# Dilated attention's logits from rounded parts stacked over 128 rows, and a new order of the branches in the mix stage of a two-block model

## The chip, the cores and the metric

One core of a Trainium2 chip runs the whole program as one launch. The metric is device time in microseconds of an execution; lower is better. The kernel before took 2573.86 us (median of 3 runs, 2573.66 to 2575.83).

Engines are named as in the profile: PE (TensorE, matrix products), ACT (ScalarE), DVE (VectorE), POOL (GpSimd), SP (SyncE, which here only issues DMAs). Each engine takes its instructions in a fixed order and waits at the first that isn't ready. ACTq, SPq and POOLq are the same engines issuing DMAs.

## The reference

A first block of two layers (three kinds of attention and memory each) is followed by a second block, on 512 tokens of width 1024 in float32. The change lies in the second block's mixing layer:

```python
def hybrid_layer_2(x, mem, ...):
    x = x + 0.5 * swiglu_ffn(rmsnorm(x, ffn1_norm), ffn1_w_in, ffn1_w_down)
    u = rmsnorm(x, mix_norm)
    u_ssm, q, k, v, xq, g_ssm, g_attn, g_mem = jnp.split(u @ w_in, cuts, axis=-1)
    y_ssm = jax.nn.gelu(s5_scan(u_ssm, ...))
    glu_a, glu_b = jnp.split(y_ssm @ ssm_w_glu, 2, axis=-1)
    br_ssm = glu_a * jax.nn.sigmoid(glu_b)
    br_attn = dilated_mixture_attention(q, k, v, rel_table) @ attn_w_up
    br_mem = memory_cross_attention(xq, rmsnorm(mem, mem_norm), xattn_w_kv) @ xattn_w_up
    merged = sigmoid(g_ssm) * br_ssm + sigmoid(g_attn) * br_attn + sigmoid(g_mem) * br_mem
    x = x + merged @ w_out
    return x + 0.5 * swiglu_ffn(rmsnorm(x, ffn2_norm), ffn2_w_in, ffn2_w_down)
```

The dilated attention has three patterns of four heads of width 64. Each query sees keys at distances 0, d, 2d, ... with d = 1, 4, 16; logits get a bias by distance. The three patterns' outputs of a head are weighted by their softmax denominators ("shares").

## The kernel before

Values are kept transposed (features on partitions, 512 tokens along the row). A large product is made of float32 operands split into a rounded high part and the rest (`hi`, `lo`, type fp32r), and of three products of 512 columns, hi x hi, hi x lo, lo x hi (`three`, lines 302 to 304). Weights come in pieces of 512 KB: SP issues the load into `raw` (line 265, two buffers), ACT rounds it (`whi`, line 270), DVE subtracts (`wlo`, line 271), three buffers each.

The mix stage runs three strands side by side, which `together` interleaves by cost: the main strand `mix_products` (projections, then gates and branch products, 256 of 1024 output features at a time), the state space (`side`, from `ssm`), and `attention` (memory's two halves, `cross`, and the dilated patterns, `dilated`, in turn). A gate is a projection and a tanh into an `fr` buffer (line 1152, four buffers). `gated` multiplies a gate with its branch and keeps the sum of branches in HBM (`mxd`, POOL's queue): place 0 writes it, place 1 reads, adds and writes it, and with `mh` the sum is rounded into the operand of the last product instead. Before, the order of branches is memory, dilated attention, and, after both side strands have ended, the state space.

`dilated` goes through 24 blocks of 128 queries and two heads (three patterns, two pairs `m`, four blocks). Per block: two logits products (one for each head, 64 rows of Q against 64 rows of K, plain fp32, line 1478), bias and minimum on DVE (line 1484), exponential on ACT (line 1486), transposes on PE (line 506), a copy on ACT (line 1492) and the value products (line 1497). An fp32 product shows as two instructions in the trace. Outputs go to HBM (`od`), maxima and sums too (`std`).

`shares` loads the statistics (`sh`), makes the weights `wt`, transposes them on PE, writes them to HBM (`wd`), loads them back over 64 partitions each (`row<-wd`, twelve DMAs on ACT's queue, four `row` buffers) and adds up the three outputs (`fr<-od`). `reload` brings a branch's input back from HBM, `fr<-yd` for memory and `fr<-sd` for the state space: a load into `fr`, an ACT cast (line 1286) and a DVE subtraction (line 1287) into `xk`.

The program's statements are scheduled ahead of time, by priority and buffers, into one fixed order for each engine.

Of the kernel before, what the change touches and what calls it, by code (L numbers as in the profile page):

```python
# [8 lines left out]
F32 = mybir.dt.float32  # L9
# [225 lines left out]
class Prog:  # L235
# [953 lines left out]
    def mix_products(self, W):  # L1189

        have = self.have
        for x in (self.cross_q(W, 0), self.dilated_qkv(W, 0), self.cross_q(W, 1), self.dilated_qkv(W, 1), self.dilated_qkv(W, 2)):
            yield from x
        x = None
        for c in range(4):
            th = self.gate(W[21 + c])
            yield 10.0
            if x is None:
                while "c1" not in have:
                    yield 0.0  # L1200
                x = self.reload(self.load_cross)
            br = self.featmajor(self.A["wxup"][c], x, nk=4)
            self.gated(c, th, br, 0)
            yield 5.0
        for c in range(4):
            th = self.gate(W[17 + c])
            yield 10.0
            while c == 0 and "oa" not in have:
                yield 0.0
            br = self.featmajor(self.A["wup"][c], self.oa, nk=2)  # L1210
            self.gated(c, th, br, 1)
            yield 3.0

    def together(self, main, streams):

        due = [0.0] * len(streams)
        for cost in main:
            for i, (gen, per) in enumerate(streams):
                due[i] += cost
                while due[i] >= per or cost == 0.0:  # L1220
                    if not next(gen, None):
                        due[i] = min(due[i], 10.0)
                        break
                    due[i] -= per
                    if cost == 0.0:
                        break
        for gen, _ in streams:
            for _ in gen:
                pass

    def mix(self):
# [4 lines left out]
        with tc.tile_pool(name="mix", bufs=1, reuse_waits="tile") as ap:  # L1236
            self.ap = ap
            with tc.tile_pool(name="ssm", bufs=1, reuse_waits="tile") as sp:
                side = self.ssm(W, sp)
                next(side)  # L1240
                z, self.hT = self.hT, self.h8(ap, "hn")
                for k in range(8):
                    q = self.row()
                    nc.vector.tensor_add(q, z[0][k].bitcast(F32), z[1][k].bitcast(F32))
                    nc.vector.tensor_mul(q, q, self.R)
                    self.split(self.hT[0][k], self.hT[1][k], q)
                self.have = set()
                self.cross_kv()
                self.together(self.mix_products(W), [(side, self.per), (self.attention(), self.aper)])
            with tc.tile_pool(name="fin", bufs=1, reuse_waits="tile") as fp:  # L1250
                mh = [[self.t(fp, [P, S], F32R, tag=f"mh{i}{d}") for d in range(8)] for i in range(2)]
                y = self.reload(self.load_ssm)
                for c in range(4):
                    pg = self.gate(W[13 + c])
                    br = []
                    for m in range(2):
                        a, b = self.featmajor(self.A["wglu"][2 * c + m], y, nk=4)
                        t = self.fr()
                        nc.scalar.activation(t, b, AF.Tanh)
                        nc.vector.scalar_tensor_tensor(t, t, 1.0, a, op0=ALU.add, op1=ALU.mult)  # L1260
                        br.append(t)
                    self.gated(c, pg, br, 2, mh)
# [35 lines left out]
    def xk(self, dt=F32R):  # L1298
        return self.t(self.ap, [P, 2, S], dt, tag="xk", bufs=6)
# [115 lines left out]
    def dilated_qkv(self, W, p):  # L1415
        nc, ap = self.nc, self.ap
        w, at, nb = self.BANDS[p]
        bias = self.m4(shape=(4, nb))
        for h in range(4):
            v = self.bd[4 * p + h][127:127 + P * (w - 1)].rearrange("(p w) -> p w", w=w - 1)  # L1420
            nc.sync.dma_start(bias[:, h, :], v[:, :nb])
        qk = []
        for x in range(2):
            ps = self.featmajor(W[2 + 3 * x + p], self.hT)
            X = self.m4()
            for m in range(2):
                src, dst = ps[m], X[:, m, :]
                if p:
                    src = src.rearrange("p (i r) -> p r i", r=4)
                    dst = dst.rearrange("p (r i) -> p r i", r=4)  # L1430
                nc.scalar.mul(dst, src, 0.125 if x == 0 else 1.0)
            qk.append(X)
            yield 10.0
# [30 lines left out]
    def dilated(self, p):  # L1464
# [6 lines left out]
        for m in range(2):  # L1471
            o = self.av()
            for b in range(NB):
                k0, n = (b * P, P) if p or b == 0 else ((b - 1) * P, 256)
                ps = [self.lt() for _ in range(2)]
                for e in range(2):
                    r = slice(64 * e, 64 * e + 64)
                    nc.tensor.matmul(ps[e][:, :n], Q[r, m, b * P:(b + 1) * P], K[r, m, k0:k0 + n], start=True, stop=True)  # L1478
                L = self.row()
                for e in range(2):  # L1480
# [3 lines left out]
                    nc.vector.tensor_tensor_reduce(Le, ps[e][:, :n], bias[:, h, nb - n:], op0=ALU.add, op1=ALU.min,  # L1484
# [21 lines left out]
    def shares(self):  # L1506
# [25 lines left out]
        acc = []  # L1532
        for p in range(3):
            for m in range(2):
                o, t = self.fr(), self.row()
# [4 lines left out]
                if p == 0:  # L1540
                    nc.vector.tensor_mul(o, o, t)
                    acc.append(o)
# [4 lines left out]
        oa = [self.xk() for _ in range(2)]  # L1547
# [212 lines left out]
    def ssm(self, W, sp):  # L1760
        nc, ap = self.nc, self.ap
        srow = lambda: self.t(sp, [P, S], tag="srow", bufs=6)
# [158 lines left out]
```

## Time and profile before

| what | value |
|---|---|
| median of 3 runs | 2573.86 us |
| the profiled execution | 2573.75 us |
| its span | 2571.9 us |
| mean granted clock of TensorE, share of full speed | 0.997 |
| two layers of the first block | 0 to 1314 us |
| first feed-forward part, state space's constants | 1314 to 1695 us |
| mix stage | 1695 to 2203 us |
| second feed-forward part and end | 2203 to 2572 us |

The stage limits are rounded readings of the timeline. A share of busy time tells which engine has little room; the waits tell where that engine stood idle, and for whom; the timeline gives the start of each instruction, and the distance from start to start is what an instruction takes of PE's time, since products overlap with the end of the one before.

### The profile page before, as it was taken

To read this page: it belongs to the slowest core of one execution; us is meant where nothing else is said; L and a number is where in the kernel's file an instruction comes from. 1 tells how busy PE (TensorE), PEld (TensorE's weight loads), DVE (VectorE), ACT (ScalarE), POOL (GpSimd) and SP (SyncE) were. 2 spreads that over 40 slices of the span, in tenths; PEclk is the share of its full clock that TensorE was granted. 3 is DMA by queue.
4 is the path that set the end of the run, shared out by engine and by line. 5 is a ranking of instruction groups with operands and counts; after the bars stand their busy time and mean duration, and the time that the engine had idled before them with its cause. 6 is when DMAs were issued, how large, how long until landed. Compare 5 with 4: busy or idle time off the path is not lost.

```text
span 2571.9 us, 33857 instructions
## 1 busy us (share of the span) xinstructions
PE 2523.3 (98%) x12104; PEld 2041.2 (79%) x12104; DVE 1675.9 (65%) x3730; ACT 1178.4 (46%) x2319; POOL 274.6 (11%) x586
## 2 busy tenths in 40 slices
PE   8999999999999999999999999999999999999998
PEld 7887777788778777778888888878876787888888
DVE  8999976554699998665489665365443445555523
ACT  7565656643466565764342332233444233333322
POOL 1010000110000000011002782000000100000000
PEclk9999999999999999999999999999999999999999
DMA  5332233343222223334333334344433544322332
GB/s 195 107 120 85 98 107 103 109 168 131 99 98 84 95 88 108 106 114 167 116 130 108 131 125 154 111 161 136 139 101 110 193 156 148 114 94 96 122 100 82
DMA packets 116880, 308.95 MB, mean 120 GB/s; under 512 B 29682, under 2 KB 37118, under 8 KB 116712
## 3 DMA queue, kind: packets, MB, share of 16 engines
q1 hardware_dynamic: 87760, 236.03, 27.7%
q0 software_dynamic: 19376, 62.30, 7.0%
q10 hardware_dynamic: 9576, 8.47, 1.0%
q8 instruction: 95, 1.56, 0.2%
q14 instruction: 73, 0.60, 0.1%
HBM read 264.72 MB, written 43.85 MB: 120 GB/s over the span
## 4 chain that ended last, share of the span: by engine, by line
PE 75%; DVE 13%; issue 7%; ACT 3%; DMA 2%; POOL 0%; SPq 0%; ACTq 0%; POOLq 0%; DVEq 0%
PE b L302 22%; PE b L303 22%; PE b L304 22%; DVE wlo L271 2%; PE b L506 2%; PE b L646 2%; DVE row L771 1%; DVE keep L620 1%; PE b L705 1%; DVE row L773 1%; DVE row L769 1%; DVE row L770 1%; DVE m L619 1%; DVE kk L754 1%; PE b L1478 1%
## 5 line engine op out<-in xcount | busy, mean ns | idle before, releaser
L271 DVE TENSOR_TENSOR wlo<-raw,whi 128x1024 fp32r<-128x1024 f32 (+1 forms) x397 | 480.9, 1211 | 486.2 <-ACT whi L270 475.1
L270 ACT CAST whi<-raw 128x1024 fp32r<-128x1024 f32 (+1 forms) x397 | 412.7, 1040 | 629.2 <-PE b L303 459.5
L302 PE MATMUL b<-h,whi 128*128 128x512 f32 x1632 | 643.1, 394 | 0.5 <-ACT h L257 0.5
L303 PE MATMUL b<-h,whi 128*128 128x512 f32 x1632 | 642.1, 393 | 0.5 <-DVE h L258 0.5
L304 PE MATMUL b<-h,wlo 128*128 128x512 f32 x1632 | 640.5, 392 | 0.0
L303 PEld LDWEIGHTS b<-h,whi 128*128 128x128 f32 x1632 | 307.5, 188 | 60.6 <-issue 1.4
L304 PEld LDWEIGHTS b<-h,wlo 128*128 128x128 f32 x1632 | 307.5, 188 | 60.7 <-issue 0.5
L302 PEld LDWEIGHTS b<-h,whi 128*128 128x128 f32 x1632 | 307.2, 188 | 60.5 <-ACT x L1720 0.7
L302 PE MATMUL b<-hn,whi 128*128 128x512 f32 x320 | 129.8, 406 | 4.2 <-ACT fr L1152 3.9
L303 PE MATMUL b<-hn,whi 128*128 128x512 f32 x320 | 128.5, 402 | 0.1
L304 PE MATMUL b<-hn,wlo 128*128 128x512 f32 x320 | 128.0, 400 | 0.0
L506 PE MATMUL b<-cst,row 128*128 128x128 f32 x452 | 87.1, 284 | 14.9 <-DVE row L773 9.7
L506 PEld LDWEIGHTS b<-cst,row 128*128 128x128 f32 x452 | 52.9, 141 | 57.5 <-issue 17.3
L1054 ACT ACTIVATE row<-row 128x512 f32<-128x512 f32 x44 | 27.8, 632 | 123.6 <-DVE row L1053 99.7
L302 PE MATMUL b<-whi,h 128*128 128x512 f32 x192 | 75.8, 395 | 0.9 <-DVE mls L806 0.9
L302 PEld LDWEIGHTS b<-hn,whi 128*128 128x128 f32 x320 | 60.8, 190 | 19.8 <-ACT fr L1152 4.3
L302 PE MATMUL b<-yb,whi 128*128 128x512 f32 x192 | 76.0, 396 | 0.0
L303 PE MATMUL b<-yb,whi 128*128 128x512 f32 x192 | 75.9, 395 | 0.0
L304 PE MATMUL b<-yb,wlo 128*128 128x512 f32 x192 | 75.5, 393 | 0.0
L304 PE MATMUL b<-whi,h 128*128 128x512 f32 x192 | 75.5, 394 | 0.0
L303 PE MATMUL b<-wlo,h 128*128 128x512 f32 x192 | 75.5, 393 | 0.0
L303 PEld LDWEIGHTS b<-hn,whi 128*128 128x128 f32 x320 | 60.7, 190 | 14.8 <-issue 1.2
(587 smaller groups left out, 4984.7 us busy)
## 6 DMA issues: line engine op xcount, KB each, us to landing
raw<-in_win_dram SPq DMA_DIRECT2D x158, 512.0 KB, 3.5
raw<-in_ffn_in_dram SPq DMA_DIRECT2D x88, 512.0 KB, 3.4
raw<-in_winw_dram SPq DMA_DIRECT2D x32, 512.0 KB, 3.7
raw<-in_ffn_down_dram SPq DMA_DIRECT2D x30, 512.0 KB, 3.6
raw<-in_wbr_dram SPq DMA_DIRECT2D x24, 512.0 KB, 3.3
mxd<-fr POOLq DMA_DIRECT2D x48, 256.0 KB, 2.4
fr<-mxd POOLq DMA_DIRECT2D x48, 256.0 KB, 3.7
raw<-in_wout_dram SPq DMA_DIRECT2D x24, 512.0 KB, 3.4
```

Source lines behind the costliest of these rows:

```text
L270: nc.scalar.copy(hi, raw)
L271: nc.vector.tensor_sub(lo, raw, hi.bitcast(F32))
L302: mm(ps, a[0], b[0], start=first, stop=False)
L303: mm(ps, a[0], b[1], start=False, stop=False)
L304: mm(ps, a[1], b[0], start=False, stop=last)
L506: self.nc.tensor.transpose(out, in_, self.c("ident"))
L619: nc.vector.max(out=m8, in_=acc)
L620: nc.vector.match_replace(out=acc, in_to_replace=m8, in_values=acc, imm_value=TAKEN)
L646: self.nc.tensor.matmul(o[:, c], V(sb), PT[i][:, sb, c], start=sb == 0 and i == 0, stop=sb == 3 and i == 1)
L705: nc.tensor.matmul(p[:, :nn], Q[h][:, tb * P:(tb + 1) * P], kk[i][:, :nn], start=i == 0, stop=i == 1)
L754: nc.vector.tensor_sub(kk[1][64 * e:64 * e + 64, :], src, kk[0][r, :].bitcast(F32))
L1054: nc.scalar.activation(th, t, AF.Tanh, scale=0.5)
```

## The change

Three things. First, the logits of the dilated attention: Q of a head is split, its high part on partitions 0 to 63 and the rest on 64 to 127. K stays in fp32, and at the start of each pair `m` it is split for each head into two tiles (`kk2`): the high part copied onto both halves, and the rest on both. Two fp32r products over 128 rows then give (Qhi + Qlo) x Khi + (Qhi + Qlo) x Klo. They are always 256 columns wide (`w0`), of which a block uses 128 or 256. Second, buffers: the bias has tiles of its own (patterns 1 and 2 share one, and pattern 2 loads it on POOL's queue), `xk` has four buffers for six, `srow` four for six, the shares' sums and outputs use `xq` tiles for `fr`, and their rounded sum `kk2`. Third, the order: memory's output is reloaded ahead of the last dilated projections, the state space's gates and products come second (with attention still running beside them), and the dilated branch comes last.

```diff
     def mix_products(self, W):
-        for x in (self.cross_q(W, 0), self.dilated_qkv(W, 0), self.cross_q(W, 1), self.dilated_qkv(W, 1), self.dilated_qkv(W, 2)):
+        for x in (self.cross_q(W, 0), self.dilated_qkv(W, 0), self.cross_q(W, 1), self.dilated_qkv(W, 1)):
             yield from x
-        x = None
+        while "c1" not in have:
+            yield 0.0
+        x = self.reload(self.load_cross)
+        yield from self.dilated_qkv(W, 2)
         for c in range(4):
             th = self.gate(W[21 + c])
...
+    def glu_products(self, W):
+        y = self.reload(self.load_ssm)
         for c in range(4):
-            th = self.gate(W[17 + c])
+            pg = self.gate(W[13 + c])
             yield 10.0
...
+            br = []
+            for m in range(2):
+                a, b = self.featmajor(self.A["wglu"][2 * c + m], y, nk=4)
+                t = self.fr()
+                self.nc.scalar.activation(t, b, AF.Tanh)
+                self.nc.vector.scalar_tensor_tensor(t, t, 1.0, a, op0=ALU.add, op1=ALU.mult)
+                br.append(t)
+                yield 5.0
+            self.gated(c, pg, br, 1)
...
-                y = self.reload(self.load_ssm)
+                self.together(self.glu_products(W), [(attention, self.aper)], [attention])
                 for c in range(4):
...
+                    th = self.gate(W[17 + c])
+                    self.gated(c, th, self.featmajor(self.A["wup"][c], self.oa, nk=2), 2, mh)
...
     def dilated_qkv(self, W, p):
-        bias = self.m4(shape=(4, nb))
+        bias = self.t(ap, [P, 4, nb], tag="bias0" if p == 0 else "bias", bufs=1)
...
-            nc.sync.dma_start(bias[:, h, :], v[:, :nb])
+            (nc.sync if p < 2 else nc.gpsimd).dma_start(bias[:, h, :], v[:, :nb])
...
+        for h in range(4):
+            src = place(ps[h // 2][64 * (h % 2):64 * (h % 2) + 64, :])
+            nc.scalar.mul(order(Q[h][0:64, :]), src, 0.125)
+            nc.vector.scalar_tensor_tensor(order(Q[h][64:128, :]), src, 0.125, order(Q[h][0:64, :]).bitcast(F32),
+                                           op0=ALU.mult, op1=ALU.subtract)
...
     def dilated(self, p):
         for m in range(2):
             o = self.av()
+            kk = []
+            for e in range(2):
+                r = slice(64 * e, 64 * e + 64)
+                k = self.t(ap, [P, 2, S], F32R, tag="kk2", bufs=2)
+                for i in range(2):
+                    nc.scalar.copy(k[64 * i:64 * i + 64, 0, :], K[r, m, :])
+                for i in range(2):
+                    nc.vector.tensor_sub(k[64 * i:64 * i + 64, 1, :], K[r, m, :], k[r, 0, :].bitcast(F32))
+                kk.append(k)
+            yield True
...
+                w0 = min(k0, 256)
                 ps = [self.lt() for _ in range(2)]
                 for e in range(2):
-                    r = slice(64 * e, 64 * e + 64)
-                    nc.tensor.matmul(ps[e][:, :n], Q[r, m, b * P:(b + 1) * P], K[r, m, k0:k0 + n], start=True, stop=True)
+                    for i in range(2):
+                        nc.tensor.matmul(ps[e][:, :256], Q[2 * m + e][:, b * P:(b + 1) * P], kk[e][:, i, w0:w0 + 256],
+                                         start=i == 0, stop=i == 1)
+                ps = [x[:, k0 - w0:k0 - w0 + n] for x in ps]
...
     def shares(self):
+        o2 = [self.t(ap, [P, 2, S], tag="xq", bufs=2) for _ in range(2)]
+        acc = [o2[0][:, m, :] for m in range(2)]
         for p in range(3):
             for m in range(2):
-                o, t = self.fr(), self.row()
+                o, t = o2[min(p, 1)][:, m, :], self.row()
...
-        oa = [self.xk() for _ in range(2)]
+        oa = [self.t(ap, [P, 2, S], F32R, tag="kk2", bufs=2) for _ in range(2)]
```

How this moves instructions is shown at three places. In these lists a row is line, operation, output, inputs and shape; x2 is two in a row. Line numbers of the changed kernel are its own (1497 is its logits line, 1507 the exponential, 1518 the value products, 1538 the shares' exponentials).

PE, within the dilated attention's last pattern; `h` are Q, K and V, `b` PSUM banks, `hn` the normed input, `cst` the identity. Before:

```order
L1478 MATMUL b_3372_17994<-h_17436,h_17301 128x128
L302 MATMUL b_3407_18144<-hn_16378,whi_18147 128x512
L303 MATMUL b_3407_18144<-hn_16382,whi_18147 128x512
L506 MATMUL b_3370_17987<-cst_58,row_17982 128x128
L304 MATMUL b_3407_18144<-hn_16378,wlo_18148 128x512
L302 MATMUL b_3407_18144<-hn_16378,whi_18147 128x512
L303 MATMUL b_3407_18144<-hn_16382,whi_18147 128x512
L1497 MATMUL b_3361_17961<-row_17990,h_17548 64x128 x2
L1478 MATMUL b_3373_17995<-h_17436,h_17301 128x128
```

The changed kernel, at the like place:

```order
L1497 MATMUL b_3528_18815<-kk_3506_18689,h_17926 128x256 x2
L302 MATMUL b_3540_18861<-xk_17900,whi_18865 128x512
L303 MATMUL b_3540_18861<-xk_17902,whi_18865 128x512
L304 MATMUL b_3540_18861<-xk_17900,wlo_18866 128x512
L1497 MATMUL b_3532_18832<-kk_3505_18684,h_17926 128x256 x2
L302 MATMUL b_3540_18861<-xk_17900,whi_18865 128x512
L303 MATMUL b_3540_18861<-xk_17902,whi_18865 128x512
L506 MATMUL b_3530_18825<-cst_58,row_18820 128x128
L304 MATMUL b_3540_18861<-xk_17900,wlo_18866 128x512
L506 MATMUL b_3530_18825<-cst_58,row_18820 128x128
```

One fp32 product of 128 columns on 64 rows is now two products of 256 columns on 128 rows; between a block's steps stand a handful of 512-column products in both, now those of the memory branch (`xk`).

ACT, from the last block's exponential to the shares' exponentials (`sh`). Before:

```order
L1486 ACTIVATE row_18661,st_3443_18335<-row_18661,st_3443_18335 128x128 x2
L1504 DMA std_110<-st_3443_18335 128x32
L1492 COPY row_18669<-b_3515_18666 128x256
L1501 COPY row_18739<-b_3481_18506 128x512
L1502 DMA od<-row_18739 128x512
L270 CAST whi_18861<-raw_18859 128x1024
L1517 ACTIVATE sh_18743<-sh_18743 128x4x4 x3
L1152 ACTIVATE fr_18735<-b_3517_18673 128x512
```

The changed kernel:

```order
L1507 ACTIVATE row_18856,st_3464_18494<-row_18856,st_3464_18494 128x128 x2
L1287 CAST xk_19002<-fr_19006 128x512
L1525 DMA std_110<-st_3464_18494 128x32
L1287 CAST xk_19002<-fr_19010 128x512
L270 CAST whi_19092<-raw_19090 128x1024
L1513 COPY row_18900<-b_3545_18897 128x256
L1522 COPY row_18904<-b_3504_18683 128x512
L1287 CAST xk_19003<-fr_19014 128x512
L1523 DMA od<-row_18904 128x512
L1287 CAST xk_19003<-fr_19018 128x512
L1538 ACTIVATE sh_18908<-sh_18908 128x4x4 x3
L270 CAST whi_19127<-raw_19125 128x1024
```

The four casts of the state space's reload (`xk<-fr`) now stand among the last block's steps, all ahead of the shares' exponentials.

SP, around the third load of the shares' statistics (`sh<-std`). Before:

```order
L265 DMA raw_18823<-in_wxup_dram 128x1024
L265 DMA raw_18859<-in_win_dram 128x1024
L265 DMA raw_18889<-in_win_dram 128x1024
L1510 DMA sh_18743<-std_110 128x4x8
L265 DMA raw_18925<-in_wup_dram 128x512
L1536 DMA fr_18775<-od 128x512
L1536 DMA fr_18781<-od 128x512
L265 DMA raw_18955<-in_win_dram 128x1024
L1536 DMA fr_18787<-od 128x512
```

The changed kernel:

```order
L265 DMA raw_19054<-in_win_dram 128x1024
L265 DMA raw_19090<-in_wglu_dram 128x1024
L1296 DMA fr_19006<-sd 128x512
L1296 DMA fr_19010<-sd 128x512
L265 DMA raw_19125<-in_wglu_dram 128x1024
L1296 DMA fr_19014<-sd 128x512
L1296 DMA fr_19018<-sd 128x512
L1531 DMA sh_18908<-std_110 128x4x8
L265 DMA raw_19170<-in_win_dram 128x1024
```

The state space's four loads (`fr<-sd`), which stood some twenty rows behind the shares, now stand ahead of the statistics' last load, with weight loads between and behind; the outputs' loads (`fr<-od`) went to `xq` and elsewhere.

## Rows read from the trace of the kernel before

**Rows 1.** Page, engines: busy us (share of the span) xinstructions.
```profile
PE 2523.3 (98%) x12104; PEld 2041.2 (79%) x12104; DVE 1675.9 (65%) x3730; ACT 1178.4 (46%) x2319; POOL 274.6 (11%) x586
```

**Rows 2.** Busy time by stage, the mix stage: us, engines, PEclk, DMA share, GB/s.
```profile
1695.00:2203.00 508.00, 500.45 (x2387) 395.80 (x2385) 254.87 (x516) 196.44 (x382) 23.94 (x44) 0.99 0.45 145
```

**Rows 3.** Waits of PE, 1695 to 2203: us in total, times, longest.
```profile
PE b L302 <- ACT fr L1152: 3.9, 1, 3.9
PE b L506 <- ACT row L1486: 1.3, 1, 1.3
PE b L302 <- ACT mh L257: 1.3, 1, 1.3
```

**Rows 4.** Busy time of two stretches, columns as in rows 2.
```profile
1940.00:1950.00 10.00, 10.00 (x41) 6.82 (x40) 4.25 (x15) 4.72 (x14) 1.08 (x2) 0.84 0.53 186
...
2010.00:2020.00 10.00, 8.23 (x29) 6.62 (x30) 6.98 (x9) 3.89 (x6) 1.10 (x2) 0.83 0.46 148
```

**Rows 5.** Timeline of ACT: start, us, engine, line, idle before it.
```profile
1994.10 1.14 ACTq L1539 DMA_DIRECT2D row<-wd  x2
...
2011.12 0.60 ACT L1152 ACTIVATE fr<-b 128x512 f32<-128x512 f32 x1 [7.97 <-DMA row<-wd]
```

**Rows 6.** Groups by shape, PE, mix stage: xcount | busy us, mean ns.
```profile
L1478 PE MATMUL b<-h,h 64*128 64x128 f32 x72 | 15.6, 323 | 0.0
...
L1478 PE MATMUL b<-h,h 64*128 64x256 f32 x24 | 8.4, 428 | 0.0
```

**Rows 7.** Timeline of PE around one product of the logits (line 1478).
```profile
1926.98 0.40 PE L304 MATMUL b<-xk,wlo 128*128 128x512 f32 x1
1927.31 0.48 PE L1478 MATMUL b<-h,h 64*128 64x128 f32 x2
1927.72 0.50 PE L302 MATMUL b<-hn,whi 128*128 128x512 f32 x1
...
1928.29 0.39 PE L304 MATMUL b<-hn,wlo 128*128 128x512 f32 x1
```

**Rows 8.** Timeline of PE, one of 256 columns.
```profile
1817.34 0.70 PE L1478 MATMUL b<-h,h 64*128 64x256 f32 x2
1817.97 0.50 PE L303 MATMUL b<-hn,whi 128*128 128x512 f32 x1
```

**Rows 9.** Timeline of PE, both heads' products in a row.
```profile
1969.35 0.49 PE L1478 MATMUL b<-h,h 64*128 64x128 f32 x4
```

**Rows 10.** Timeline of PE, the memory attention's logits (`xk`, `xq`).
```profile
1726.98 0.40 PE L304 MATMUL b<-hn,wlo 128*128 128x512 f32 x1
1727.22 0.28 PE L302 MATMUL b<-xk,xq 128*128 128x256 f32 x1
1727.34 0.27 PE L303 MATMUL b<-xk,xq 128*128 128x256 f32 x1
...
1728.08 0.39 PE L304 MATMUL b<-hn,wlo 128*128 128x512 f32 x1
```

**Rows 11.** Groups by shape, ACT and DVE: the stick attention's rounded K.
```profile
L752 ACT CAST kk<-r 64x512 fp32r<-64x512 f32 x32 | 19.8, 619 | 6.5 <-PE b L761 6.1
...
L754 DVE TENSOR_TENSOR kk<-r,kk 64x512 fp32r<-64x512 f32 x32 | 21.8, 682 | 0.8 <-ACT kk L752 0.2
```

**Rows 12.** DMA issues (count, KB, us to landing); then the chain of waits.
```profile
fr<-sd SPq DMA_DIRECT2D x4, 256.0 KB, 3.5
...
2061.25 5.69 DMA fr<-sd
...
2066.97 1.13 ACT xk L1286
```

**Rows 13.** Timelines of ACT and DVE at the shares.
```profile
1987.59 0.43 ACT L1517 ACTIVATE sh<-sh 128x16 f32<-128x16 f32 x3 [1.58 <-DVE sh L1516]
...
1988.86 0.35 DVE L1525 TENSOR_TENSOR wt<-sh,shs 128x16 f32<-128x16 f32 x3
```

**Rows 14.** Waits of PE, whole span: transposes of the stick attention.
```profile
PE b L506 <- DVE row L773: 9.7, 26, 0.8
```

More of the change, by code (lines that the diff above doesn't have):

```diff
@@ L1197, in mix_products @@
             yield 10.0
[L1198 to L1201, printed above, removed]
             br = self.featmajor(self.A["wxup"][c], x, nk=4)
@@ L1204, in mix_products, with together @@
             yield 5.0
+    def glu_products(self, W):
+        y = self.reload(self.load_ssm)
         for c in range(4):
-            th = self.gate(W[17 + c])
+            pg = self.gate(W[13 + c])
             yield 10.0
[L1208 to L1214, printed above, removed]
+            br = []
[7 more added lines that the diff above has]
+            self.gated(c, pg, br, 1)
+    def together(self, main, streams, ends=()):
         due = [0.0] * len(streams)
@@ L1226, in together @@
                         break
-        for gen, _ in streams:
+        for gen in ends:
             for _ in gen:
@@ L1248, in mix @@
                 self.cross_kv()
-                self.together(self.mix_products(W), [(side, self.per), (self.attention(), self.aper)])
+                attention = self.attention()
+                self.together(self.mix_products(W), [(side, self.per), (attention, self.aper)], [side])
             with tc.tile_pool(name="fin", bufs=1, reuse_waits="tile") as fp:
                 mh = [[self.t(fp, [P, S], F32R, tag=f"mh{i}{d}") for d in range(8)] for i in range(2)]
-                y = self.reload(self.load_ssm)
+                self.together(self.glu_products(W), [(attention, self.aper)], [attention])
                 for c in range(4):
[L1254 to L1262, printed above, removed]
+                    th = self.gate(W[17 + c])
+                    self.gated(c, th, self.featmajor(self.A["wup"][c], self.oa, nk=2), 2, mh)
                 x = [self.xk(F32) for _ in range(4)]
@@ L1298, in xk @@
     def xk(self, dt=F32R):
-        return self.t(self.ap, [P, 2, S], dt, tag="xk", bufs=6)
+        return self.t(self.ap, [P, 2, S], dt, tag="xk", bufs=4)
     def m4(self, dt=F32, shape=(2, S)):
@@ L1417, in dilated_qkv @@
         w, at, nb = self.BANDS[p]
-        bias = self.m4(shape=(4, nb))
+        bias = self.t(ap, [P, 4, nb], tag="bias0" if p == 0 else "bias", bufs=1)
         for h in range(4):
             v = self.bd[4 * p + h][127:127 + P * (w - 1)].rearrange("(p w) -> p w", w=w - 1)
-            nc.sync.dma_start(bias[:, h, :], v[:, :nb])
[L1422 to L1433, printed above, removed]
+            (nc.sync if p < 2 else nc.gpsimd).dma_start(bias[:, h, :], v[:, :nb])
+        order = (lambda x: x.rearrange("p (r i) -> p r i", r=4)) if p else (lambda x: x)
+        place = (lambda x: x.rearrange("p (i r) -> p r i", r=4)) if p else (lambda x: x)
+        Q = [self.m4(F32R) for _ in range(2)]
+        Q = [Q[h // 2][:, h % 2, :] for h in range(4)]
+        ps = self.featmajor(W[2 + p], self.hT)
+        for h in range(4):
[3 more added lines that the diff above has]
+                                           op0=ALU.mult, op1=ALU.subtract)
+        yield 10.0
+        ps = self.featmajor(W[5 + p], self.hT)
+        K = self.m4()
+        for m in range(2):
+            nc.scalar.copy(order(K[:, m, :]), place(ps[m]))
+        qk = Q, K
+        yield 10.0
         if p == 0:
@@ L1483, in dilated @@
                     st = st2[:, b, 0, h:h + 1]
-                    nc.vector.tensor_tensor_reduce(Le, ps[e][:, :n], bias[:, h, nb - n:], op0=ALU.add, op1=ALU.min,
+                    nc.vector.tensor_tensor_reduce(Le, ps[e], bias[:, h, nb - n:], op0=ALU.add, op1=ALU.min,
                                                    accum_out=st, scale=-1.0, scalar=3.0e38)
@@ L1541, in shares @@
                     nc.vector.tensor_mul(o, o, t)
-                    acc.append(o)
                 else:
@@ L1761, in ssm @@
         nc, ap = self.nc, self.ap
-        srow = lambda: self.t(sp, [P, S], tag="srow", bufs=6)
+        srow = lambda: self.t(sp, [P, S], tag="srow", bufs=4)
         for c in range(2):
```

1 line of the change is left out of this document (removed).

## The prediction

> **What bounds the kernel now.** I read the page first, then the busy time by stage, then the waits of TensorE. PE is busy 2523.3 us, 98% of the span [rows 1]. The profiled execution took 2573.75 us, 1.85 us more than its span; the median of the runs, 2573.86, is 0.1 us away, so I work from 2573.75 and correct nothing. Everything that the change touches lies in the mix stage, which I take as 1695 to 2203 us; there PE is busy 500.45 of 508.00, VectorE 254.87 and ScalarE 196.44 [rows 2]. So two things can shorten it: less work on PE, or fewer of the few idle microseconds. Work on ScalarE and VectorE costs nothing until PE has to wait for it.
>
> The idle time is in three places. PE's waits of this stage [rows 3] are 3.9 us for a gate's tanh (line 1152), 1.3 us for an exponential of the dilated attention (line 1486) and 1.3 us for the rounding of the merged tensor (`mh`). What is left, single waits of 0.2 or 0.3 us, I leave out of the sum. After two of the three the clock fell: the granted clock was 0.84 over the ten microseconds from 1940 and 0.83 over those from 2010 [rows 4], against 1.00 elsewhere. That is 10 x 0.16 + 10 x 0.17 = 3.3 us lost at the lower of the two levels. Idle and clock together: 3.9 + 1.3 + 1.3 + 3.3 = **9.8 us**.
>
> Why the long one is there: ScalarE issues the twelve loads of the shares' weights (`row<-wd`, 1.14 us for two [rows 5]) from its own queue, with four `row` buffers; VectorE frees these only once the branch outputs (`fr<-od`) have landed, which themselves wait for `fr` buffers. The tanh that PE waits for stood behind that and came after 7.97 us of idle ScalarE [rows 5].
>
> **The change part by part.**
> *Logits on PE.* There are 48 products per head and block. In fp32 each is two instructions, 72 of 128 columns and 24 of 256 [rows 6]. What one costs is read from starts. Alone: from L304 at 1926.98 to L304 at 1928.29 is 1.31 us, and three steps of 512-column products (0.232 each) belong to others, so 0.61 us [rows 7]. Of that, 0.41 us lie between its own start and the next (1927.31 to 1927.72) and 0.20 around it; next to another fp32 product (values, transposes) that neighbour pays the 0.20 anyway, and I count 0.41. Of 256 columns the stretch between the starts is 0.63 us (1817.34 to 1817.97) [rows 8], so alone 0.63 + 0.20 = 0.83. The second head of a pair placed directly behind the first is free: x4 lasts 0.49 us [rows 9], x2 0.48. Going through PE's order of before, of 36 with 128 columns 20 stand alone, 12 next to an fp32 product and 4 behind another; of 12 with 256 columns 6 and 6. Sum: 20 x 0.61 + 12 x 0.41 + 6 x 0.83 + 6 x 0.63 = **25.9 us**.
> After, each is two fp32r products of 256 columns and 128 rows: 96. The trace has such products in the memory attention's logits: from 1726.98 to 1728.08 three of them run among three 512-column steps, 1.10 - 0.70 = 0.40, so 0.135 us each [rows 10]. 96 x 0.135 = 13.0 us. **Saved: 12.9 us.** The first of the three took 0.12 (1727.22 to 1727.34); were two so cheap, the third took 0.16. With 0.12 or 0.16 for all, 14.4 or 10.5 us are saved.
>
> *Making the parts.* 24 rounding copies on ScalarE and 24 subtractions on VectorE of 64x512, like the stick attention's `kk`, 0.619 and 0.682 us [rows 11]: 14.9 and 16.4 us; the stacked Q adds about 3.5 us on ScalarE and 8.3 us on VectorE. Both engines are under 51% busy [rows 2], so I cost this at nothing in sum. It can show where a half of the heads begins (a new `kk2` pair stands between PE's last logits and the next): five such borders, four operations of 0.65 us each deep with other products in between: 1 us taken, 0 to 3.
>
> *Memory's output reloaded early.* The loads `fr<-yd` now stand before the last dilated projections, so weights don't wait behind them on SP's queue at the moment that the gates need them. The 1.3 us and the clock after it go. The wait for "c1" now holds the main stream instead; attention has nothing else to wait for there, so 0 (0 to 1.5).
>
> *Shares with their own buffers, and other work beside them.* The branch outputs no longer need `fr`, and PE has the state space's branch (gates and `wglu`) to do instead of waiting for `oa`. The 3.9 us and their clock go. The merge's rounding is now behind `wup`, with partial sums read well ahead: the 1.3 us at `mh` go too.
>
> *What comes in their place: the shares' transposes (A).* In the new order of PE they stand 27 products of 512 columns, two transposes and a pair of value products behind the last memory product (call its end T): PE gets there at T + 27 x 0.232 + 0.8 = T + 7.05. Their operand `wt` waits for VectorE and ScalarE, where the four reloads of the state space's output now stand in front of the shares' exponentials. The third reload needs the buffer that VectorE's subtraction of the first frees, at about T + 1.2. From there the load, 3.5 us in the median and 5.69 us for the one on the chain; two casts of 1.13 us and a subtraction of about the same [rows 12]; the exponentials, and from these to `wt` 1.6 us as now (1987.59 to 1988.86 and 0.35) [rows 13], with one of 0.5 us more for what VectorE does between them. Sum T + 1.2 + 3.5 + 3 x 1.13 + 1.6 + 0.5 = T + 10.2. PE waits 3.1 us; with the long load 5.3 (2.2 more); if loads land early 0. A wait of that size brought the low clock above, 1.7 us. **4.8 us, 0 to 7.**
> *(B)* Then ScalarE issues the twelve `row<-wd`, 0.57 us each [rows 5], with two weight casts between, and a gate's tanh stands behind them; PE needs its bank 58 products (13.5 us) after the transposes. Twelve issues are 6.8 us, the wait for `wd` and for two row buffers some 5: 0.8 taken, 0 to 2.5 (the nearest row is the 3.9 of before, whose `fr` buffers are out of it).
> *(C)* The third pattern's bias is now loaded on POOL's queue into the buffer that the second leaves, after its last logits; four loads, queued behind partial sums: 0.3, 0 to 2.
>
> Net: -12.9 - 9.8 + 4.8 + 0.8 + 0.3 + 1.0 = **-15.8 us**, so 2573.75 - 15.8 = 2557.95, **2558**.
>
> **The rivals.**
> *(1) Stalls only move.* A, B, C and the borders take near their upper ends, 10 to 16 us against the 9.8 that go: then little but the logits is gained, 2573.75 - 12.9 - 9.8 + 11 to 16 = 2562 to 2567. For it: four loads, casts and loads again stand in one line on in-order queues. Against: PE has 7 us of independent products there, and the `fr` buffers are out of it.
> *(2) No new stall.* Transposes in time: -12.9 - 9.8 and 1 to 2 us at B, C and the borders, 2552; with the logits' good end 2549. It needs the reload to run during the last block, but the buffers speak against it.
> *(3) Pairs were cheap.* If both heads' products had run side by side throughout, stacking gives that up. An adjacent pair does so: four instructions in the time of two [rows 7, 9]. Were all 24 pairs of before like that, they would cost 18 x 0.61 + 6 x 0.83 = 16.0 us, the saving would be 3.0, and the time 2573.75 - 3.0 - 9.8 + 6.9 = 2567.9. But only 4 of 48 stand so. By the page "TensorEngine Tiling (Array Packing)" of the Trainium skill, section Key Properties, tiles on different partitions load weights and multiply in parallel, which speaks against stacking two parts over all 128 rows; the adjacent pair agrees, the order of the program hardly uses it.
> *(4) The dilated blocks become paced by ScalarE and VectorE* (the slower side). Each of 24 blocks goes logits, bias and exponential, transposes, copy, values, with few products between in PE's order. Where copies of `kk2` and weight casts stand in front of the exponential, PE waits at the transposes. The like of it in the stick attention cost 9.7 us in 26 waits, 0.37 each and 0.8 at most [rows 14]. It eats the 15.8 us from 0.66 us a block on, and makes the kernel slower by over 5.1 us from (15.8 + 5.1)/24 = 0.87 us a block on: 2579 and more. The casts fall only at borders, five of 24, so every block would have to be late: unlikely.
>
> **How the numbers follow.** 0.2% is 5.1 us, about what a measurement of this kernel can tell from no change. Forecast (2552 to 2562): 0.58. Rival 1 (2562 to 2567): 0.17. Rival 2 (2549 to 2552): 0.08. Rival 3: 0.05, 2566 to 2570. Rival 4: 0.12, of which 0.07 slower than 2579 and 0.05 near no change. The range reaches from 2548 (all new costs zero and 14.4 us of logits: 2573.75 - 14.4 - 9.8 = 2549.6, and 1.4 us for the small waits left out) to 2568 (A to C and borders at 16 us, 2573.75 - 12.9 - 9.8 + 16 = 2567.1; or at 14 with the logits' poor end, 2567.5). Faster by over 0.2% is up to 2568.6: 0.58 + 0.17 + 0.08 + 0.03 = 0.86, less 0.02 for costs that I don't see: 0.84. Same 0.09, slower 0.07.
>
> **What the profile would show.** The logits: a row of fp32r products of 128x256, x96, and none in fp32; PE's busy time in the mix stage lower by about 13 us. Stall 1 gone: no wait for line 1486's successor at memory's first product. Stall 2: no wait of several microseconds for a gate's tanh behind `row<-wd`. A: a wait of PE's transposes for `wt` of about 3 us, and one stretch of lower clock behind it. Borders: waits for `kk2` under 1 us in sum. The prediction is wrong if `wt` comes late by more than 5 us, if waits at line 506 add up over the blocks, or if the 96 products take over 0.2 us each.

## The result, and the profile after

The changed kernel took 2560.59 us (median of 4 runs, 2558.96 to 2561.91) against 2574.72 us before on the same chip: ratio 0.9945, 95% interval 0.9933 to 0.9956. That is 14.1 us less, where the prediction had 15.8 less and a range of 2548 to 2568. In a later session it was 2563.97 against 2576.16 (0.9950, 0.9938 to 0.9963), 12.2 us less. The profiled execution took 2561.91 us, the longest of its four, with a span of 2560.1 us: 11.8 us under the span before.

First the row of the page with the engines, then the mix stage's row of the busy times by stage (columns as in [rows 1] and [rows 2]; the stage now ends near 2191).

```profile
PE 2511.7 (98%) x12104; PEld 2039.1 (80%) x12104; DVE 1700.3 (66%) x3766; ACT 1196.6 (47%) x2349; POOL 272.6 (11%) x590
```

```profile
1695.00:2191.00 496.00, 488.29 (x2392) 393.57 (x2390) 279.42 (x554) 214.62 (x413) 26.10 (x48) 1.00 0.46 149
```

PE is busy 488.29 us for 500.45 [rows 2], 12.2 us less; VectorE 24.6 and ScalarE 18.2 us more, as worked out. Outside this stage PE's busy time is within 0.6 us of before. The idle time of PE is hardly less. Its waits in the mix stage (us in total, times, longest):

```profile
PE b L302 <- DVE fr L1216: 2.6, 1, 2.6
PE b L302 <- ACT fr L1152: 1.7, 1, 1.7
PE b L506 <- DVE wt L1546: 1.4, 1, 1.4
PE b L302 <- ACT row L1379: 1.0, 1, 1.0
```

None of the three of [rows 3] is there in its old place. Four others are: 2.6, 1.7, 1.4 and 1.0 us, and a small one of 0.2 at the value products. And there is one stretch of lower clock again (the granted clock is the third figure from the end, 0.83):

```profile
2010.00:2020.00 10.00, 7.43 (x26) 5.63 (x25) 9.41 (x14) 2.68 (x4) 0.68 (x2) 0.83 0.43 141
```

So the stage lost 9.8 us of old waits and slow clock, got 2.6 + 1.7 + 1.4 + 1.0 + 0.2 and 1.7 us of lower clock (10 x 0.17) = 8.6 us of new, and the rest of its gain is the logits. Their group by shape (xcount | busy, mean ns):

```profile
L1497 PE MATMUL b<-kk,h 128*128 128x256 f32 x96 | 21.9, 309 | 0.0
```

By the starts in the trace, 96 of these take 14.1 us of PE, 0.147 each. What they replace I take from all stretches of fp32 products between two fp32r ones, from 1722 us to the end of the attention, measured from the start of the product ahead to the start of the second behind, less those two products' own steps: 98 stretches with 78.6 us before, 92 with 53.4 us after. Each of the two sums holds one wait of the transposes, 1.3 and 1.4 us, so these cancel. 78.6 - 53.4 - 14.1 = **11.1 us saved**. With the waits, -11.1 - 9.8 + 8.6 = -12.3, against 11.8 measured in the two profiled executions.

### The profile page after: what moved, and what is told of

Its sections match the earlier page's. It is cut to its first block, busy times and chain, and to the rows that moved or that the text cites. A ratio compares the mean times of both kernels' runs of the same rounds, so it can differ in the third digit from the quotient of the medians.

```text
span 2560.1 us, 33922 instructions
## 1 busy us (share of the span) xinstructions
PE 2511.7 (98%) x12104; PEld 2039.1 (80%) x12104; DVE 1700.3 (66%) x3766; ACT 1196.6 (47%) x2349; POOL 272.6 (11%) x590
## 5 line engine op out<-in xcount | busy, mean ns | idle before, releaser
L302 PEld LDWEIGHTS b<-hn,whi 128*128 128x128 f32 x320 | 60.7, 190 | 16.1 <-DVE fr L1216 3.0
L303 PEld LDWEIGHTS b<-hn,whi 128*128 128x128 f32 x320 | 60.6, 189 | 13.9 <-DVE hn L258 0.7
```

Of the source, the lines that this page charges most:

```text
L302: mm(ps, a[0], b[0], start=first, stop=False)
L303: mm(ps, a[0], b[1], start=False, stop=False)
```

## The experiments

Two questions were open: do the logits and the order each give what these sums say, and what makes the new waits? Each kernel ran beside the kernel before; I give the difference from it on the same chip, since the sessions ran on different chips and differ by a microsecond or two. The changed kernel stands at -14.1 and -12.2 us.

**Logits without the new order.** The order of `mix_products` and of the `fin` part is put back; logits and buffers stay.

```diff
-        for x in (self.cross_q(W, 0), self.dilated_qkv(W, 0), self.cross_q(W, 1), self.dilated_qkv(W, 1)):
+        for x in (self.cross_q(W, 0), self.dilated_qkv(W, 0), self.cross_q(W, 1), self.dilated_qkv(W, 1), self.dilated_qkv(W, 2)):
             yield from x
-        while "c1" not in have:
-            yield 0.0
-        x = self.reload(self.load_cross)
-        yield from self.dilated_qkv(W, 2)
+        x = None
...
-                self.together(self.glu_products(W), [(attention, self.aper)], [attention])
+                y = self.reload(self.load_ssm)
...
+                    self.gated(c, pg, br, 2, mh)
```

> The changed logits and buffers, with the order of branches of the kernel before. Theory (the logits save 11 us on PE by the islands of fp32 products, the new order by itself only exchanges stalls of about 10 us for stalls of about 9): 2574.7 - 11 = 2564, between 2561 and 2566, with waits of the old kind (a gate's tanh behind the loads of the shares' weights, memory's late reload) of 8 to 10 us with their clock. Rival (making the rounded parts costs PE several us, the order brings the gain): 2568 to 2573.

Measured: 2576.66 us against 2575.56, ratio 1.0006 (0.9996 to 1.0015). **No gain at all**: neither theory nor rival. PE's longest waits in the mix stage, then two rows of ten microseconds each (clock third from the end):

```profile
PE b L302 <- ACT kk L257: 6.1, 1, 6.1
PE b L302 <- ACT mh L257: 4.2, 1, 4.2
PE b L506 <- ACT row L1507: 2.9, 3, 1.7
```

```profile
2010.00:2020.00 10.00, 3.94 (x11) 2.56 (x10) 5.73 (x8) 1.24 (x2) 0.00 (x0) 0.71 0.37 95
...
2160.00:2170.00 10.00, 10.00 (x36) 7.94 (x35) 4.91 (x7) 3.44 (x5) 1.09 (x2) 0.78 0.43 142
```

The 96 products cost 13.9 us there, as little as in the changed kernel, but waits and the lower clock take up what they save. PE waits 6.1 us for `oa`, the sum of the shares, a wait that the kernel before does not have; 4.2 us for the merged tensor, where it waited 1.3 [rows 3]; and 2.9 us for exponentials of the dilated attention, for 1.3. All listed waits of the stage come to 16.1 us, for 7.2 before, and five windows of ten microseconds with a lower clock lose 1.7 + 2.9 + 0.5 + 1.2 + 2.2 = 8.5 us for 3.3.

That PE simply comes earlier to operands that are late does not explain the two longest waits. For `oa` the order of PE has moved too: between the shares' transposes and the first product that needs `oa` stand 54 products of lines 302 to 304, and 79 before, while the way from these transposes to the first cast of `oa` took no longer (20.1 us for 22.0). The dilated strand ends later in the order: 1015 such products of the stage stand ahead of its last logits, for 942 before (1010 in the changed kernel). A likely reason is that `dilated` now hands over once more for each pair (`yield True` ahead of the blocks, six times in all); no run takes these away. At the merged tensor PE arrived only 0.7 us earlier than before (2155.1 for 2155.7), but the load of a partial sum ahead of it took longer. Before, then here:

```profile
2151.78 3.80 DMA fr<-mxd
```

```profile
2151.11 6.72 DMA fr<-mxd
```

**The new order without the logits.** Q and K are made and multiplied in fp32 as before; buffers of the bias, reloads and branch order stay as changed.

```diff
-                    for i in range(2):
-                        nc.tensor.matmul(ps[e][:, :256], Q[2 * m + e][:, b * P:(b + 1) * P], kk[e][:, i, w0:w0 + 256],
-                                         start=i == 0, stop=i == 1)
+                    r = slice(64 * e, 64 * e + 64)
+                    nc.tensor.matmul(ps[e][:, :n], Q[r, m, b * P:(b + 1) * P], K[r, m, k0:k0 + n], start=True, stop=True)
```

> The changed kernel with the plain fp32 logits of before (bias, buffers and order as changed). Theory: 2560.6 + 11 = 2571.5, between 2569 and 2574, that is 1 to 5 us under the kernel before. Rival (the order brings most of the gain): 2562 to 2567.

Measured: 2573.22 against 2575.56, -2.3 us (0.9988, 0.9978 to 0.9997). By itself the order exchanges waits: the three of [rows 3] are gone, and two at the shares have come.

```profile
PE b L302 <- DVE fr L1216: 2.6, 1, 2.6
PE b L302 <- ACT fr L1215: 1.4, 1, 1.4
```

Together these two make a table. Beside the difference in time stands what the profiled executions show of the stage, from its first product on `hn` to the last on `mh`: its length, PE's idle time in it, what the lower clock cost (half of the time at that level), and the rest, which is PE's work (us).

| kernel | time | stage | idle | clock | rest |
|---|---|---|---|---|---|
| before | 0 | 478.7 | 7.4 | 3.4 | 467.9 |
| logits alone | +1.1 | 481.0 | 16.6 | 8.5 | 455.9 |
| order alone | -2.3 | 475.1 | 5.6 | 1.7 | 467.8 |
| both | -14.1 and -12.2 | 465.8 | 7.6 | 1.7 | 456.5 |

The logits take 11 to 12 us off PE's work with either order. **Only with the new order does this saving reach the time**: with the old one it is lost to waits and to the lower clock. In the changed kernel 405 products stand between the shares' transposes and the first that needs `oa`, for the 54 of the logits alone. Both kernels of this test keep the new buffers and the six hand-overs, so it is not shown that the logits would gain nothing in the order of before without these.

**Memory's early reload alone taken back.**

```diff
-        while "c1" not in have:
-            yield 0.0
-        x = self.reload(self.load_cross)
         yield from self.dilated_qkv(W, 2)
+        x = None
         for c in range(4):
             th = self.gate(W[21 + c])
             yield 10.0
+            if x is None:
+                while "c1" not in have:
+                    yield 0.0
+                x = self.reload(self.load_cross)
```

> The changed kernel with memory's output reloaded at the first memory gate, as before the change. Theory (the early reload took away the wait of 1.3 us at memory's first product and the 1.7 us of lower clock behind it): both return, 2562 to 2565. Rival (the state space's branch in second place does all of the order's work): 2559.5 to 2561.5.

Measured: 2568.45 against 2575.28, -6.8 us (0.9971, 0.9960 to 0.9983), 5 to 7 us worse than the changed kernel, more than expected. PE's waits, then the ten microseconds from 1930:

```profile
PE b L302 <- ACT fr L1152: 3.0, 1, 3.0
PE b L506 <- ACT row L1509: 2.9, 3, 1.7
...
1930.00:1940.00 10.00, 8.78 (x27) 6.09 (x27) 4.19 (x9) 5.29 (x16) 0.00 (x0) 0.66 0.29 89
```

PE waits three times for an exponential (line 1509 here), 2.9 us in all; the longest, 1.7 us, stands at memory's first products (1931), and behind it the granted clock over ten microseconds is 0.66: 3.4 us, twice the loss of before. The stage is 6.0 us longer than in the changed kernel (471.8 for 465.8), so the early reload is worth some 6 us, about half of the gain. What makes the exponential late there is not shown.

**What makes the new waits.** In the changed kernel ScalarE and then VectorE are blocked at the shares. Timeline of ScalarE, then of VectorE (start, us, operation, idle before it):

```profile
2002.92 3.94 ACTq L1561 DMA_DIRECT2D row<-wd  x4
2006.91 0.60 ACT L1152 ACTIVATE fr<-b 128x512 f32<-128x512 f32 x1 [3.02 <-DMA row<-wd]
...
2006.13 1.08 DVE L1566 TENSOR_TENSOR row<-xq,row 128x512 f32<-128x512 f32 x1 [3.30 <-DMA row<-wd]
...
2010.72 1.07 DVE L1566 TENSOR_TENSOR row<-xq,row 128x512 f32<-128x512 f32 x1
2011.82 0.69 DVE L1567 TENSOR_TENSOR xq<-xq,row 128x512 f32<-128x512 f32 x1
2012.43 0.68 DVE L1216 SCALAR_TENSOR_TENSOR fr<-fr,b 128x512 f32<-128x512 f32 x1
```

The tanh of a gate (line 1152) stood behind the last issues of `row<-wd` until 2006.91; PE got its bank 1.7 us late. Then a multiplication of the state space's branch (line 1216, 2012.43) stood behind three of the shares' sums: the first of them had VectorE idle for 3.30 us until its `row<-wd` landed (2006.13), and from there VectorE worked without a pause. That gave the 2.6 us. One landing of `row<-wd` on the chain of waits was long:

```profile
2000.01 6.02 DMA row<-wd
```

To test that it is the place in the queues, `shares` became a generator that hands over after each step, so that the scheduler can put gates and branch products between.

```diff
-        self.oa = self.shares()
+        yield from self.shares()
...
         nc.scalar.dma_start(self.wd, wr[0:12, :])
+        for _ in range(2):
+            yield True
...
                     nc.vector.tensor_add(acc[m], acc[m], t)
+                for _ in range(2):
+                    yield True
```

> The changed kernel with the shares' last part emitted in steps, so that a gate's tanh and the state space's products no longer stand behind all twelve loads and six sums. Theory (the waits of 1.7 and 2.6 us for lines 1152 and 1216 and the 1.7 us of lower clock behind them come from that block): 2554 to 2557. Rival (the loads' landing of up to 6 us or the weights are the cause, the place in the queues is not): 2559 to 2562.

Measured: 2556.65 against 2575.56, -18.9 us (0.9927, 0.9912 to 0.9942). The waits that are left, and ScalarE's and VectorE's rows at that place:

```profile
PE b L506 <- DVE wt L1546: 1.4, 1, 1.4
PE b L302 <- ACT row L1379: 1.0, 1, 1.0
PE b L302 <- DVE fr L1216: 0.3, 1, 0.3
```

```profile
2000.57 0.59 ACT L1152 ACTIVATE fr<-b 128x512 f32<-128x512 f32 x1
2001.02 2.57 ACTq L1563 DMA_DIRECT2D row<-wd  x4
...
2010.31 0.68 DVE L1216 SCALAR_TENSOR_TENSOR fr<-fr,b 128x512 f32<-128x512 f32 x1
```

The tanh now runs at 2000.57 between the issues, the multiplication at 2010.31 between the sums. Both waits are gone but for 0.3 us, and so is the slow stretch. In the later session, five rounds each:

> The changed kernel once more, as the neighbour on the same chip for the three that follow: 2559 to 2562.

> Shares in steps, against the changed kernel on the same chip. Theory (two waits of PE and the lower clock behind them gone, as its first trace showed): 3 to 6 us below the changed kernel, 2555 to 2558. Rival (the first difference was scatter between chips): within 1.5 us of it.

The changed kernel 2563.97, the one in steps 2556.77, against 2576.16: -12.2 and -19.4 us (0.9950 and 0.9923, 0.9910 to 0.9937). There the changed kernel's wait for the tanh was 2.9 us, where the kernel in steps waited 0.7 at line 1216:

```profile
PE b L302 <- ACT fr L1152: 2.9, 1, 2.9
```

```profile
PE b L506 <- DVE wt L1546: 1.3, 1, 1.3
PE b L302 <- ACT row L1379: 1.0, 1, 1.0
PE b L302 <- DVE fr L1216: 0.7, 1, 0.7
```

So the block is the cause of these two waits, and **the shares in steps beat both kernels**, by 7.2 us here, more than expected. In the two profiled executions the stage is 4.0 us shorter (460.3 for 464.3), which is the waits and the clock; the rest of the 7.2 is not accounted for, and the five runs in steps spread over 6 us.

**Loads of the shares' weights on another queue.** `nc.scalar.dma_start` of the twelve loads becomes `nc.gpsimd.dma_start`, first in the changed kernel, then in the one in steps.

> The changed kernel with the twelve loads of the shares' weights issued from POOL's queue instead of ScalarE's. Theory (two separate blocks, ScalarE's by the issues and VectorE's by the sums that wait for landings): the wait of 1.7 us for a tanh goes, the one of 2.6 us for line 1216 stays with its clock: 2558 to 2560. Rival (one block only, in ScalarE's queue): both go, 2554 to 2556.

Measured: 2559.46 against 2575.56, -16.1 us (0.9936, 0.9921 to 0.9951). The wait for the tanh is gone, the one for line 1216 is there, as two separate blocks would have it:

```profile
PE b L302 <- DVE fr L1216: 2.2, 1, 2.2
```

> Shares in steps and the loads of their weights from POOL's queue. Theory (steps alone already take the block away; 0.3 us of it were left): within 1 us of the shares in steps. Rival (ScalarE still loses time to issuing): 1 to 3 us below it.

Measured: 2557.85 against 2576.16, -18.3 us; that is 1.1 us longer than the steps alone, and within the scatter. No further gain: ScalarE's issues are no longer in the way.

**Is the making of the parts hidden?** Each rounding copy and subtraction of K made twice.

```diff
-                for i in range(2):
+                for i in (0, 1, 0, 1):
                     nc.scalar.copy(k[64 * i:64 * i + 64, 0, :], K[r, m, :])
-                for i in range(2):
+                for i in (0, 1, 0, 1):
                     nc.vector.tensor_sub(k[64 * i:64 * i + 64, 1, :], K[r, m, :], k[r, 0, :].bitcast(F32))
```

> The changed kernel with each rounding copy and subtraction of the parts of K made twice (24 more of 0.6 us on ScalarE, 24 of 0.7 us on VectorE). Theory (the making of the parts lies beside other work): within 2 us of the changed kernel, 2559 to 2562.5. Rival (the parts hold PE up at the borders between pairs of heads, and are why the saving is smaller than the forecast): 2564 and more, with waits of PE at the logits.

Measured: 2565.15 against 2575.28, -10.1 us (0.9957, 0.9943 to 0.9972), 2 to 4 us worse than the changed kernel, its four runs spread over 5 us. PE's waits:

```profile
PE b L302 <- ACT fr L1152: 3.3, 1, 3.3
...
PE b L1518 <- ACT row L1513: 1.2, 2, 1.0
...
PE b L1497 <- DVE kk L1487: 0.5, 2, 0.3
```

At the logits themselves PE waits 0.5 us for 31 us of added work on the two engines, so the borders are covered; but the time is the rival's, not the theory's, and 1.0 us came at value products. Against the changed kernel's first profile the stage is 2.1 us longer (467.9 for 465.8), and nearly all of that is the lower clock behind the tanh wait at the shares' block, 3.4 us for 1.7:

```profile
2010.00:2020.00 10.00, 7.07 (x19) 5.59 (x20) 9.36 (x12) 3.25 (x5) 0.00 (x0) 0.66 0.47 144
```

That place is open to scatter: the tanh wait of 3.3 us here was 1.7 and 2.9 us in two runs of the changed kernel. Whether the doubled work made it longer I can't tell from this run.

**Fewer columns.** Logits as wide as the block uses, 128 columns for 72 of the 96.

> The changed kernel with fp32r logits only as wide as the block uses: 72 of the 96 products have 128 columns for 256. If a product's time follows its columns (0.147 us for 256 in the changed kernel), 72 x 0.06 = 4 us go: 2555 to 2558. If 128 columns cost as much as 256: 2560 to 2562. If they cost more, as the fp32 ones did (0.41 us for one of 128 columns in two instructions): 72 x 0.06 or more is added, 2565 and up.

Measured: 2562.98 against 2575.28, -12.3 us, like the changed kernel. Groups by shape, and a wait that is new:

```profile
L1497 PE MATMUL b<-kk,h 128*128 128x128 f32 x72 | 13.2, 273 | 0.2 <-DVE st L1505 0.2
...
L1497 PE MATMUL b<-kk,h 128*128 128x256 f32 x24 | 5.8, 319 | 0.0
```

```profile
PE b L506 <- ACT row L1507: 1.7, 5, 0.4
```

By starts, those of 128 columns take 0.121 us each and those of 256 columns 0.156 in this kernel: 72 x 0.026 = 1.9 us less than at 0.147, not 4. PE's work in the stage, counted as in the table above, is no smaller (458.0 for 456.5), and there are five short waits of the transposes for the exponential, 1.7 us. Where the 1.9 us went is open; that the blocks come up against ScalarE with less between them is a guess.

**The reload behind the shares.** In the kernel in steps, the state space's output is reloaded after its first gate, so that its casts don't stand ahead of the shares' exponentials.

```diff
-        y = self.reload(self.load_ssm)
+        y = None
         for c in range(4):
             pg = self.gate(W[13 + c])
+            if y is None:
+                y = self.reload(self.load_ssm)
```

> Shares in steps, and the state space's output reloaded after its first gate. Theory (the four casts ahead of the shares' exponentials cause the 1.4 us at the shares' transposes; PE's gate covers the reload): the wait for wt goes, 2554.5 to 2556. Rival (the wait only moves to the first product that needs the reloaded output): 2556.5 to 2561.

Measured: 2565.72 against 2575.28, -9.6 us, longer than theory and rival had it. The wait for `wt` is gone, but products wait 7.6 us for the reloaded tensor, and a clock of 0.66 over ten microseconds behind that costs 3.4 us more:

```profile
PE b L302 <- ACT xk L1289: 5.3, 2, 4.5
PE b L303 <- DVE xk L1290: 2.3, 2, 1.8
```

The reload's place ahead of the shares is the better one.

**Two of its subtractions on GpSimd**, in the kernel in steps: `tensor_sub` of `reload` on `nc.gpsimd` for the third and fourth part.

> Shares in steps, and two of the four subtractions of the state space's reload on GpSimd. Theory (VectorE's subtractions of about 1.1 us stand ahead of the shares' steps and make the 1.4 us at the shares' transposes): that wait falls to 0.3 us or none, 1 us below the shares in steps. Rival (the third load of the statistics lands too late by itself): the wait stays over 1 us.

Measured: 2559.09 against 2576.16, -17.1 us, 2.3 us longer than in steps. The wait for `wt` grew to 2.9 us, and a stretch of lower clock (0.83, 1.7 us) is back:

```profile
PE b L506 <- DVE wt L1546: 2.9, 1, 2.9
```

VectorE's timeline, then GpSimd's:

```profile
1989.38 1.19 DVE L1535 TENSOR_TENSOR shm<-shm,sh 128x16 f32<-128x16 f32 x1 [1.70 <-DMA sh<-std]
1990.61 1.61 DVE L1537 TENSOR_TENSOR sh<-shm,sh 128x16 f32<-128x16 f32 x3
...
1988.98 3.04 POOL L1288 TENSOR_TENSOR xk<-fr,xk 128x512 fp32r<-128x512 f32 x2 [2.57 <-ACT xk L1287]
```

And the same two steps of VectorE in the changed kernel:

```profile
1989.02 0.16 DVE L1535 TENSOR_TENSOR shm<-shm,sh 128x16 f32<-128x16 f32 x1
1989.21 0.35 DVE L1537 TENSOR_TENSOR sh<-shm,sh 128x16 f32<-128x16 f32 x3
```

One step of 16 elements took 1.19 us and three took 1.61, for 0.16 and 0.35, while GpSimd subtracted. So this test doesn't tell whether the subtractions on VectorE cost the 1.4 us; that stays open.

## Why the prediction was right, and where its steps were off

Direction and size held (14.1 us for 15.8, and 12.2 in the later session), but by parts that partly cancel: the logits gave 1.8 us less than forecast, A cost 3.4 us less, B 5.2 us more. That so little of this shows in the sum is luck.

- *Logits*: forecast 12.9 us saved, measured 11.1. The new products took 0.147 us and not 0.135, which is 1.1 us; the old ones were 0.7 us cheaper than their sum. PE's work in the stage, less idle time and clock, fell by 11.4 us, which agrees.
- *The old waits*: 9.8 us, all gone. But the sum adds the logits and the waits as if each came by itself. The table above shows that they don't: order alone gains 2.3 us, and with the old order the logits gain nothing. Of what takes their saving there, the 4.2 us are an old wait grown, by a slower load, and the 6.1 us are a new one. The prediction had no rival for it; as the change held both parts, it didn't cost the forecast anything.
- *A, the shares' transposes*: forecast a wait of 3.1 us and 1.7 us of clock, measured 1.4 us and no slow clock. The chain is the forecast one, casts and subtractions of the reload ahead of the exponentials, on ScalarE and then VectorE:

```profile
1987.88 1.12 ACT L1287 CAST xk<-fr 128x512 fp32r<-128x512 f32 x1
1989.43 0.43 ACT L1538 ACTIVATE sh<-sh 128x16 f32<-128x16 f32 x3 [0.42 <-DVE sh L1537]
...
1989.48 1.10 DVE L1288 TENSOR_TENSOR xk<-fr,xk 128x512 fp32r<-128x512 f32 x1
...
1991.49 0.35 DVE L1546 TENSOR_TENSOR wt<-sh,shs 128x16 f32<-128x16 f32 x3
```

  From the last memory product (1983.1) `wt` took 8.8 us for 10.2, and PE needed 7.5 us to get there for 7.05. The load was 2.7 us (1984.15 to 1986.86), not 3.5.
- *B, ScalarE's twelve issues*: this is the step that failed. Forecast 0.8 us, 2.5 at most; measured 1.7 + 2.6 + 1.7 of clock = 6.0 us (2.9 + 1.7 = 4.6 in the second run). The first issue came 4.2 us after the transposes (1991.98 to 1996.15), behind `wd`'s write, and the tanh 14.9 us after them, for the 13.5 that PE left. And the same block was not looked for on VectorE, where a multiplication of the branch that PE was working on stands behind the sums. Rival 1, stalls that only move, was half right: the new costs came to 8.6 us, between the forecast's 6.9 and the rival's 10 to 16.
- *The borders*: 1 us forecast, no wait for `kk2` seen; with the parts made twice such waits came to 0.5 us. Instead Q's alternating steps on ScalarE and VectorE stood ahead of an exponential of the memory attention (line 1379), for which PE waited 1.0 us at 1889:

```profile
1886.28 0.59 ACT L1431 ACTIVATE h<-b 64x512 fp32r<-64x512 f32 x1 [0.88 <-DVE h L1432]
...
1888.37 0.59 ACT L1431 ACTIVATE h<-b 64x512 fp32r<-64x512 f32 x1
1888.99 0.47 ACT L1379 ACTIVATE row<-b,xst 128x256 f32<-128x256 f32 x1
```

  The kernel with fp32 logits, which has no such steps, lacks this wait. So does the one with narrow logits, which has them; that the steps alone cause it is not shown.
- *C, the bias on POOL's queue*: 0.3 us forecast, no wait seen.
- Rival 3, pairs side by side, fell with the 11.1 us; by the Trainium skill's page "TensorEngine Tiling (Array Packing)", section Key Properties, the rows' halves can work in parallel, and the trace shows it only for adjacent pairs [rows 9]. Rival 4, blocks paced by ScalarE and VectorE, didn't come; the five short waits with 128 columns, 1.7 us, are the nearest to it.
- *Two sums*: rival 2's 2549 us leaves out the 1 to 2 us of new costs that it names; with them it is 2550.6 at least. The small waits that the range counts at 1.4 us come to 0.7 in the list of waits. Neither changes the forecast.

## What to carry to other kernels

Work taken off the busiest engine shortens the time only as far as no new wait takes its place: test the parts of a change apart and together, since here two parts of +1 and -2 us made -14. Split the stage into that engine's work, its idle time and its clock, which shows where a saving went. See too whether an edit moves the order of the strands, as one more hand-over in each pair may have done here. When a side task of long loads ends in one piece, look on every in-order engine that it uses for what the main strand has queued behind it, and hand it over in steps.

## What the runs showed of the hardware

- An fp32r product's time falls less than its columns: 0.232 us for 512, 0.147 for 256 in the changed kernel, and 0.156 for 256 and 0.121 for 128 in the one with narrow logits, by starts among other products.
- The lower of TensorE's two clock levels (1.2 GHz) came behind some waits of PE and not behind others, and not by their length. Over ten microseconds, 0.84 followed a wait of 1.3 us in the kernel before, 0.83 one of 2.9 us in the changed kernel's second run (1.6 and 1.7 us lost), and 0.66 one of 1.7 us in the kernel with the late memory reload (3.4 us lost). The 1.4 us at `wt` gave no drop, and neither did a tanh wait of 3.0 us in the kernel with the late reload.
- VectorE's steps took longer while GpSimd subtracted (two operations, 3.04 us). That agrees with the Trainium skill's page "Trainium Architecture — The Big Picture", section What this means for kernel authors, by which these two engines contend for a shared pair of ports under an exclusive lock. Here even a step of 16 elements took 1.19 us for 0.16.
